# Last four input transposes of FFN-up moved into its first panel, and the fourth pair of weight halves in FFN-down given to other steps

## The chip, the cores and the metric

The kernel runs on one core of one Trainium2 chip. The metric is device time in microseconds, the median of three runs; lower is better. TensorE (PE) multiplies, VectorE (DVE), ScalarE (ACT) and GpSimd (POOL) work on its operands and results, and SyncE (SP) issues most loads.

## The reference, cut to what matters

One decoder layer over 256 tokens of width 2048: a mixer (a pooling part and an RWKV-7 part), an MLP, a gated embedding and a last norm. The change touches the MLP and the step into it:

```python
mix = jnp.concatenate([pool_out, rwkv_out], axis=-1).astype(x.dtype)
x = x + mix @ w_out[i]

h2 = rms_norm(x, mlp_norm[i])
x = x + jnp.square(jax.nn.relu(h2 @ w_ffn_up[i])) @ w_ffn_down[i]   # 2048 -> 8192 -> 2048

gate = jax.nn.sigmoid(rms_norm(x, ple_norm[i]) @ w_ple_gate[i])
x = x + gate * (p[i] @ w_ple_proj[i])
return rms_norm(x, final_norm)
```

## The kernel before, in words

All products are made from float32 values split in two halves, a high one (wh, from an ACT copy into float32r) and a low one (wl, from a DVE subtraction); each product of two split operands takes three matmuls. Weights arrive as raw tiles of 128x1024 (load_raw, line 158, on SP's queue), in two groups of three buffers, are split by ACT and DVE, and then read by TensorE. The tiles wh and wl rotate through three shared buffers each (pool wp). The splits have a high priority (20000), so that they are made as early as buffers and data allow. Order on each engine is decided by a scheduler when the program is built; the code gives program order and priorities. Each engine then works through its own list in that order, and an instruction that waits holds up all behind it on its engine.

**The way into FFN-up.** The output product runs in four column blocks n (gemm_toks, lines 238 to 242); after each, residual (line 1071) adds the block to x on DVE, and h2_part("mlp_norm", n) makes four of the 16 column tiles of h2: for each pair of tiles four transposes on TensorE (line 1134) into half of a two-bank PSUM tile (wide_bank, pool psw with two buffers), and per tile one evacuation on ACT (line 1140, high half) and one on DVE (line 1141, low half). The scale 1/rms is applied later, on the squared result.

**FFN-up** (gemm_wide) runs in 16 panels, eight for each half of the hidden width. A panel has two half panels, and each half panel runs through four quarters kq over the inner width: one raw load, one split (lines 167 and 168), and sixteen matmuls, in groups of two on wh with both halves of h2 (line 1112, 512 columns) and two on wl (line 1117, 256 columns). Quarter kq reads the column tiles 4 kq to 4 kq + 3 of h2. square (lines 1356 to 1358) then evacuates the wide PSUM tile, and begin_sum and activation_sums prepare FFN-down.

**FFN-down** (down_sweep, two sweeps in each half) goes over 16 row blocks kp. Half of them (SEVEN) are done in seven products in place of eight, a Strassen scheme, and are called squares here. A plain block splits its two raw loads by halves_of, giving the pairs a and b. A square has the pair a, a pair b that holds the halves of one raw load (w22) and of a sum from the ring (w1), a pair wad (from the ring less w22, line 1313), and a pair d made from raw weights that were changed in place (line 1315). The ring has two slots; a slot is filled by two DMAs of POOL, the second adding to what the first brought (lines 1232 and 1233), and the first two fills start during FFN-up, in panels 4 and 5.

The pairs a and b get their tiles from half_tiles (line 1266). It counts its calls in turns, and every fourth gets a pair of its own (wh4, wl4, one buffer each), the others the three shared buffers. A sweep has 32 calls, the last one 37. So the fourth call of each sweep, which is pair b of the first square (wh_d_1b, wl_d_1b), has the own pair.

Of the kernel before, what the change touches and what calls it, by code (L numbers as in the profile page):

```python
# [16 lines left out]
T = 256  # L17
# [23 lines left out]
def trunk(  # L41
# [29 lines left out]
    def mm_bank(name):  # L71
        return psm.tile([128, 512], F32, tag="mm", name=name)
# [12 lines left out]
    def col(name, j):  # L85
        o = PARAM_COLS[name] + j
        return par_sb[:, o : o + 1]
# [7 lines left out]
    ident = const.tile([128, 128], F32, name="ident")  # L95
# [53 lines left out]
    def load_raw(src, n, name):  # L149
        own = False  # L150
        if deep:
            deep.append(name)
            own = len(deep) > 5 and len(deep) % 6 < 3
        if own:
            raw = fp.tile([128, 1024], F32, tag="raw2", bufs=3, name=f"raw_{name}")
        else:
            raw = wp.tile([128, 1024], F32, tag="raw", name=f"raw_{name}")
        nc.sync.dma_start(raw[:, 0:n], src)
        return raw

    def split_w(raw, name):

        wh = wp.tile([128, 1024], F32R, tag="wh", name=f"wh_{name}")
        wl = wp.tile([128, 1024], F32R, tag="wl", name=f"wl_{name}")
        with tc.high_priority(20000):
            for a in range(2):
                nc.scalar.activation(wh[:, a * 512 : (a + 1) * 512], raw[:, a * 512 : (a + 1) * 512], AF.Copy)  # L167
            nc.vector.tensor_tensor(wl, raw, wh.bitcast(F32), op=ALU.subtract)  # L168
        return [(t_h, t_l) for t_h, t_l in zip((wh[:, 0:512], wh[:, 512:1024]), (wl[:, 0:512], wl[:, 512:1024]))]

    def split_sb(h_ap, l_ap, src_ap):
        nc.scalar.activation(h_ap, src_ap, AF.Copy)  # L172
        nc.vector.tensor_tensor(l_ap, src_ap, h_ap.bitcast(F32), op=ALU.subtract)
# [111 lines left out]
    def run(gen):  # L285
        for _ in gen:
            pass

    def a8(slot, name, dt=F32):
        return act.tile([128, 2048], dt, tag=f"a{slot}", name=name)  # L290
# [768 lines left out]
    xr = [a8(3 + tt, f"x{tt}") for tt in range(2)]  # L1059
# [7 lines left out]
    def residual(banks, n):  # L1067
        for tt in range(2):
            xs = xr[tt][:, n * 512 : (n + 1) * 512]
            with tc.high_priority(30000):  # L1070
                nc.vector.tensor_tensor(xs, banks[tt], xs, op=ALU.add)
# [23 lines left out]
    def wide_bank(name):  # L1095
        return psw.tile([128, 2, 512], F32, tag="wide", name=name)

    def gemm_wide(src, acts, name, consume):

        for half in range(2):
            bank = wide_bank(f"{name}_w{half}")
            for kq in range(4):
                raw = load_raw(src[half, kq].rearrange("p a n -> p (a n)"), 1024, f"{name}{half}_{kq}")
                for a, (wh, wl) in enumerate(split_w(raw, f"{name}{half}_{kq}")):
                    for b in range(2):
                        k = kq * 4 + 2 * a + b
                        hl = acts(k)
                        cs = [slice(b * 256 + ct * 128, b * 256 + ct * 128 + 128) for ct in range(2)]  # L1110
                        for ct in range(2):
                            nc.tensor.matmul(  # L1112
                                bank[:, ct, :].rearrange("p (s t) -> p s t", s=2), wh[:, cs[ct]], hl,
                                start=k == 0, stop=False, skip_group_check=True,
                            )
                        for ct in range(2):
                            nc.tensor.matmul(  # L1117
                                bank[:, ct, 0:T], wl[:, cs[ct]], hl[:, 0, :], start=False, stop=k == 15, skip_group_check=True
                            )
            consume(half, bank)  # L1120

    def transposed(name):

        hl = fp.tile([128, 2, NK, T], F32R, tag="h2", name=name)
        h, l = hl[:, 0], hl[:, 1]

        def part(norm, n):
            for j2 in range(2 * n, 2 * n + 2):
                if j2 % 2 == 0:
                    b = wide_bank(f"{name}t")  # L1130
                for jj in range(2):
                    j = 2 * j2 + jj
                    for tt in range(2):
                        nc.tensor.transpose(
                            b[:, j2 % 2, jj * T + tt * 128 : jj * T + (tt + 1) * 128], xr[tt][:, j * 128 : (j + 1) * 128], ident
                        )
                for jj in range(2):
                    j = 2 * j2 + jj
                    src = b[:, j2 % 2, jj * T : (jj + 1) * T]
                    nc.scalar.activation(h[:, j, :], src, AF.Copy, scale=col(norm, j))  # L1140
                    nc.vector.scalar_tensor_tensor(
                        l[:, j, :], src, col(norm, j), h[:, j, :].bitcast(F32), op0=ALU.mult, op1=ALU.subtract
                    )

        return part, lambda k: hl[:, :, k, :]

    h2_part, h2 = transposed("h2")
    deep.append("w_out")
    for n in range(4):
        run(gemm_toks(w_out[n], mix, f"o{n}", lambda banks: residual(banks, n), (6, 7, 2, 3)))  # L1150
        h2_part("mlp_norm", n)


    s2 = const.tile([128, 2], F32, name="s2sq")
# [1 line left out]
    def inv_ms():  # L1156
        ss2 = rms_stat(xr, "n2")
        nc.vector.tensor_scalar(s2, ss2, 1.0 / D, NORM_EPS, op0=ALU.mult, op1=ALU.add)
        nc.vector.reciprocal(s2, s2)
        nc.vector.tensor_scalar_mul(ns2, s2, -1.0)  # L1160
# [57 lines left out]
    turns = []  # L1218
# [4 lines left out]
    def begin_sum(after=None):  # L1223

        n = len(begun)
        if not ring:
            ring.append(fp.tile([128, 1024], F32, tag="S", name="ring"))
        if n < len(in_line):
            hf, pair, kp = in_line[n]
            if after is not None:  # L1230
                nc.gpsimd.tensor_copy(slot(n)[:, 0:1], after[:, 0:1])
            nc.gpsimd.dma_start(slot(n), w_down[pair, hf * 16 + kp, 1, :, 1, :])  # L1232
            nc.gpsimd.dma_start(slot(n), w_down[pair, hf * 16 + kp, 0, :, 1, :], accum_op=ALU.add)  # L1233
            begun.append(n)
# [4 lines left out]
    def down_sweep(hf, pair, ys, sboxes, hooks=(), between=None):  # L1239
# [26 lines left out]
        def half_tiles(name):  # L1266

            turns.append(name)
            if len(turns) % 4 == 0:
                return [fp.tile([128, 1024], F32R, tag=f"{hl}4", name=f"{hl}_{name}") for hl in ("wh", "wl")]  # L1270
            return [wp.tile([128, 1024], F32R, tag=hl, name=f"{hl}_{name}") for hl in ("wh", "wl")]

# [20 lines left out]
        for q, kp in enumerate(visits):  # L1293
            if q in hooks:
                hooks[q]()
            y, j = ys[kp // 2], kp % 2 * 512
            a11, a21, a12, a22 = ((y[:, j + i * 128 : j + i * 128 + 128], y[:, 1024 + j + i * 128 : 1152 + j + i * 128]) for i in range(4))
            rx, ry = (panel(kp, c, f"{nm}_{kp}_{c}", 1 if c and kp in seven else 2) for c in range(2))
            if kp in seven:
                i = SEVEN.index(kp)  # L1300
# [27 lines left out]
            if kp == max(seven):  # L1328
                u = fp.tile([128, 512], F32, tag="r", bufs=2, name=f"u{nm}")
# [16 lines left out]
    def ffn_half(hf):  # L1346
        sboxes = {}
        ys = []
        for i in range(8):
            f = hf * 8 + i  # L1350
            y = fp.tile([128, 2048], F32R, tag="y", bufs=8, name=f"y{f}")

            def square(bi, bank):
                r = fp.tile([128, 512], F32, tag="r", bufs=2, name=f"r{f}_{bi}")
                r2 = r.rearrange("p (c t) -> p c t", c=2)
                nc.scalar.activation(r2, bank[:, :, T : 2 * T], AF.Copy)
                nc.vector.tensor_tensor(r2, bank[:, :, 0:T], r2, op=ALU.add)
                nc.vector.scalar_tensor_tensor(r, r, 0.0, r, op0=ALU.max, op1=ALU.mult)  # L1358
                split_sb(y[:, bi * 512 : bi * 512 + 512], y[:, 1024 + bi * 512 : 1024 + bi * 512 + 512], r)
                if f in (4, 5) and bi:  # L1360
                    begin_sum(r)
                if 2 * i + bi in SEVEN:
                    activation_sums(sboxes, 2 * i + bi, r)

            gemm_wide(w_up[f], h2, f"u{f}", square)
            ys.append(y)
            if f == 1:
                inv_ms()

        if hf == 1:  # L1370
            h3_part, h3 = transposed("h3")
            h3_box.append(h3)

        down_sweep(hf, 0, ys, sboxes)
        if hf == 0:
            down_sweep(hf, 1, ys, sboxes)
        else:
            down_sweep(hf, 1, ys, sboxes, {5: keep, 8: keep, 11: keep, 14: keep}, lambda: [h3_part("ple_norm", n) for n in range(2)])
            for n in range(2, 4):
                h3_part("ple_norm", n)  # L1380
# [24 lines left out]
    part = const.tile([128, 1], F32, name="part")  # L1405
# [131 lines left out]
```

## Time and profile before

| | us |
|---|---|
| median of three runs | 1180.53 |
| lowest and highest | 1179.17 and 1183.03 |
| time of the profiled execution | 1182.91 |
| its span, first to last instruction | 1181.1 |
| TensorE, busy (share of the span) | 1162.8 (98%) |
| DVE, ACT, POOL, busy | 877.7, 714.1, 58.5 |
| mean granted clock of TensorE | 0.995 |

Times inside the profile count from the start of its span. A row of a timeline gives start, duration, engine, line, operation, output and inputs, shape, and how often it stands in one row (x2); in square brackets follows how long the engine sat idle before it, and for whom it waited. Numbers of buffers are left out of names (u_w, wh_d_0a), so a name stands for all of a kind. Matmuls overlap: one takes 0.39 us from start to end where the next starts 0.23 us after it. FFN-up's first half runs from 378 to 563 us, FFN-down's first two sweeps to 727, the second half of both to 1072. The windows give for each stretch the busy time and the number of instructions of each engine, then the granted clock of TensorE, the DMA share and the rate.

### The profile page before, as it was taken

To read this page: it belongs to the slowest core of one execution; us is meant where nothing else is said; L and a number is where in the kernel's file an instruction comes from. 1 tells how busy PE (TensorE), PEld (TensorE's weight loads), DVE (VectorE), ACT (ScalarE), POOL (GpSimd) and SP (SyncE) were. 2 spreads that over 40 slices of the span, in tenths; PEclk is the share of its full clock that TensorE was granted. 3 is DMA by queue.
4 is the path that set the end of the run, shared out by engine and by line. 5 is a ranking of instruction groups with operands and counts; after the bars stand their busy time and mean duration, and the time that the engine had idled before them with its cause. 6 is when DMAs were issued, how large, how long until landed. Compare 5 with 4: busy or idle time off the path is not lost.

```text
span 1181.1 us, 17409 instructions
## 1 busy us (share of the span) xinstructions
PE 1162.8 (98%) x6407; PEld 973.1 (82%) x6407; DVE 877.7 (74%) x1194; ACT 714.1 (60%) x1323; POOL 58.5 (5%) x133
## 2 busy tenths in 40 slices
PE   9999999999999999999999999999999999999997
PEld 8787777788887888878888888888888888888886
DVE  8686996954656676757888988676768988897543
ACT  8777858676545565545665664555556665677543
POOL 2100000000000000000110110000000110000000
PEclk9999999999999999989999999999999999999999
DMA  8454443354454555555687686555555886975511
GB/s 294 154 199 144 142 143 109 119 179 161 175 190 171 179 190 191 198 171 204 202 241 244 200 245 233 194 182 194 186 189 174 248 250 228 316 247 190 198 56 72
DMA packets 67253, 224.42 MB, mean 190 GB/s; under 512 B 7712, under 2 KB 8480, under 8 KB 66784
## 3 DMA queue, kind: packets, MB, share of 16 engines
q1 hardware_dynamic: 60240, 207.38, 50.2%
q0 software_dynamic: 6496, 15.21, 5.7%
q8 instruction: 50, 0.82, 0.3%
q10 hardware_dynamic: 432, 0.73, 0.2%
q14 instruction: 35, 0.29, 0.1%
HBM read 221.19 MB, written 2.10 MB: 189 GB/s over the span
## 4 chain that ended last, share of the span: by engine, by line
PE 93%; DVE 3%; DMA 2%; ACT 2%; issue 1%; POOL 0%; SPq 0%; DVEq 0%; POOLq 0%; ACTq 0%
PE u_w L1112 19%; PE u_w L1117 10%; PE d_b L1262 7%; PE d_b L1264 7%; PE d_b L1263 7%; PE d_w L1262 2%; PE d_w L1264 2%; PE d_w L1263 2%; PE gt_b L238 2%; PE gt_b L241 2%; PE gt_b L242 2%; PE o_b L241 1%; PE o_b L242 1%; PE zv_b L238 1%; PE o_b L238 1%; PE zp_b L238 1%
## 5 line engine op out<-in xcount | busy, mean ns | idle before, releaser
L1112 PE MATMUL u_w<-h,wh_u 128*128 128x512 f32 x1024 | 323.8, 398 | 1.8 <-ACT wh_u L167 1.8
L167 ACT ACTIVATE wh_u<-raw_u 128x512 fp32r<-128x512 f32 x256 | 147.4, 623 | 154.9 <-issue 95.5
L168 DVE TENSOR_TENSOR wl_u<-raw_u,wh_u 128x1024 fp32r<-128x1024 f32 x128 | 156.7, 1224 | 104.6 <-ACT wh_u L167 102.9
L1117 PEld LDWEIGHTS u_w<-h,wl_u 128*128 128x128 f32 x1024 | 193.6, 189 | 47.2 <-DVE wl_u L168 1.5
L1117 PE MATMUL u_w<-h,wl_u 128*128 128x256 f32 x1024 | 202.6, 279 | 0.9 <-DVE wl_u L168 0.9
L1112 PEld LDWEIGHTS u_w<-h,wh_u 128*128 128x128 f32 x1024 | 157.0, 190 | 2.0 <-ACT wh_u L167 2.0
L168 DVE TENSOR_TENSOR wl_gt<-raw_gt,wh_gt 128x1024 fp32r<-128x1024 f32 x24 | 29.4, 1224 | 23.2 <-ACT wh_gt L167 23.1
L172 ACT ACTIVATE wad<-ring 128x512 fp32r<-128x512 f32 x29 | 18.2, 629 | 43.1 <-DVE ring L1313 43.1
L167 ACT ACTIVATE wh_gt<-raw_gt 128x512 fp32r<-128x512 f32 x48 | 28.0, 639 | 23.0 <-PE gt_b L242 14.4
L241 PE MATMUL gt_b<-wh_gt,h 128*128 128x512 f32 x96 | 37.3, 389 | 0.0
L242 PE MATMUL gt_b<-wh_gt,h 128*128 128x512 f32 x96 | 37.3, 389 | 0.0
L1315 DVE TENSOR_TENSOR raw_d<-raw_d,ring 128x1024 f32<-128x1024 f32 x29 | 35.5, 1222 | 0.7
L1232 POOL DMA_DIRECT2D ring<-in_w_ffn_down_dram x29 | 16.5, 570 | 356.8 <-DVE r L1358 190.8
L1233 POOL DMA_DIRECT2D ring<-in_w_ffn_down_dram x29 | 25.4, 876 | 110.4 <-DMA ring<-in_w_ffn_down_dram 110.4
L168 DVE TENSOR_TENSOR wl_o<-raw_o,wh_o 128x1024 fp32r<-128x1024 f32 x16 | 19.6, 1223 | 12.9 <-ACT wh_o L167 11.4
L167 ACT ACTIVATE wh_o<-raw_o 128x512 fp32r<-128x512 f32 x32 | 18.4, 623 | 16.3 <-issue 8.5
L167 ACT ACTIVATE wh_zp<-raw_zp 128x512 fp32r<-128x512 f32 x32 | 18.6, 624 | 15.8 <-PE zp_b L242 7.1
L168 DVE TENSOR_TENSOR wl_zk<-raw_zk,wh_zk 128x1024 fp32r<-128x1024 f32 x16 | 19.4, 1220 | 9.8 <-ACT wh_zk L167 9.8
L241 PE MATMUL zv_b<-wh_zv,hTh 128*128 128x512 f32 x64 | 26.0, 406 | 0.0
L241 PE MATMUL zk_b<-wh_zk,hTh 128*128 128x512 f32 x64 | 25.2, 394 | 0.6 <-ACT wh_zk L167 0.6
L241 PE MATMUL zp_b<-wh_zp,hTh 128*128 128x512 f32 x64 | 25.7, 401 | 0.0
L238 PE MATMUL gt_b<-wl_gt,h 128*128 128x512 f32 x96 | 25.7, 389 | 0.0
(927 smaller groups left out, 3007.2 us busy)
## 6 DMA issues: line engine op xcount, KB each, us to landing
raw_u<-in_w_ffn_up_dram SPq DMA_DIRECT2D x128, 512.0 KB, 3.5
raw_d<-in_w_ffn_down_dram SPq DMA_DIRECT2D x99, 512.0 KB, 4.7
ring<-in_w_ffn_down_dram POOLq DMA_DIRECT2D x58, 256.0 KB, 4.5
raw_gt<-in_w_ple_gate_dram SPq DMA_DIRECT2D x24, 512.0 KB, 3.5
raw_zk<-in_w_in_dram SPq DMA_DIRECT2D x16, 512.0 KB, 3.7
raw_zr<-in_w_in_dram SPq DMA_DIRECT2D x16, 512.0 KB, 3.3
raw_zv<-in_w_in_dram SPq DMA_DIRECT2D x16, 512.0 KB, 3.3
raw_zp<-in_w_in_dram SPq DMA_DIRECT2D x16, 512.0 KB, 3.2
```

The lines of the kernel that those rows point to most:

```text
L167: nc.scalar.activation(wh[:, a * 512 : (a + 1) * 512], raw[:, a * 512 : (a + 1) * 512], AF.Copy)
L168: nc.vector.tensor_tensor(wl, raw, wh.bitcast(F32), op=ALU.subtract)
L238: nc.tensor.matmul(banks[tt], ah[:, ts_], halves[a][1], start=False, stop=last)
L241: nc.tensor.matmul(banks[tt], ah[:, ts_], halves[a][0], start=i + a == 0, stop=False)
L242: nc.tensor.matmul(banks[tt], al[:, ts_], halves[a][0], start=False, stop=False)
L1112: nc.tensor.matmul(bank[:, ct, :].rearrange("p (s t) -> p s t", s=2), wh[:, cs[ct]], hl, start=k == 0, stop=False, skip_group_check=True,)
L1117: nc.tensor.matmul(bank[:, ct, 0:T], wl[:, cs[ct]], hl[:, 0, :], start=False, stop=k == 15, skip_group_check=True)
L1233: nc.gpsimd.dma_start(slot(n), w_down[pair, hf * 16 + kp, 0, :, 1, :], accum_op=ALU.add)
L1262: nc.tensor.matmul(banks[n], ah, wh, start=first, stop=False)
L1263: nc.tensor.matmul(banks[n], ah, wl, start=False, stop=False)
L1264: nc.tensor.matmul(banks[n], al, wh, start=False, stop=last)
L1315: nc.vector.tensor_tensor(t43, t43, t2.unsqueeze(1).to_broadcast([128, 2, 512]), op=ALU.subtract)
```

## The change

There are two edits. The first takes the last block of transposes out of the loop over n and calls it from gemm_wide, in the very first half panel of FFN-up, between the first and the second quarter; there it uses two plain one-bank tiles of the pool psm (mm_bank) in place of one wide tile. The second lets half_tiles give its own pair to calls 1, 5, 9 and so on in place of 4, 8, 12.

```diff
-    def gemm_wide(src, acts, name, consume):
+    def gemm_wide(src, acts, name, consume, first=None):
         for half in range(2):
             bank = wide_bank(f"{name}_w{half}")
             for kq in range(4):
+                if first is not None and half == 0 and kq == 1:
+                    first()
                 raw = load_raw(src[half, kq].rearrange("p a n -> p (a n)"), 1024, f"{name}{half}_{kq}")
...
-        def part(norm, n):
+        def part(norm, n, pair=None):
             for j2 in range(2 * n, 2 * n + 2):
-                if j2 % 2 == 0:
+                if pair is not None:
+                    b = pair[j2 % 2].unsqueeze(1)
+                elif j2 % 2 == 0:
                     b = wide_bank(f"{name}t")
+                at = 0 if pair is not None else j2 % 2
...
     for n in range(4):
         run(gemm_toks(w_out[n], mix, f"o{n}", lambda banks: residual(banks, n), (6, 7, 2, 3)))
-        h2_part("mlp_norm", n)
+        if n < 3:
+            h2_part("mlp_norm", n)
+
+    def h2_rest():
+        h2_part("mlp_norm", 3, [mm_bank(f"h2t{i}") for i in range(2)])
...
             turns.append(name)
-            if len(turns) % 4 == 0:
+            if len(turns) % 4 == 1:
                 return [fp.tile([128, 1024], F32R, tag=f"{hl}4", name=f"{hl}_{name}") for hl in ("wh", "wl")]
...
-            gemm_wide(w_up[f], h2, f"u{f}", square)
+            gemm_wide(w_up[f], h2, f"u{f}", square, h2_rest if f == 0 else None)
```

What the scheduler makes of it is shown at three places. In the changed kernel the lines behind 1098 have other numbers: 1137 is the transpose, 1285 the split in halves_of, 1363 the evacuation in square.

On TensorE, from the last matmul of the output product (o_b) into FFN-up (u_w), before; wh_u_0 and wl_u_0 are the halves of the first quarter, wh_u_1 those of the second, and h2t is the transposes' tile:

```order
L238 MATMUL o_b_3652<-wl_o_3_3713,mp_3213 128x512
L1134 MATMUL h2t<-ident,x_2724 128x128
L1112 MATMUL u_w_3751<-h_3359,wh_u_0_3754 128x512 x2
L1117 MATMUL u_w_3751<-h_3359,wl_u_0_3755 128x256
L1134 MATMUL h2t<-ident,x_2725 128x128
```

And the same place now:

```order
L238 MATMUL o_b_3652<-wl_o_3_3713,mp_3213 128x512
L1112 MATMUL u_w_3734<-h_3359,wh_u_0_3737 128x512 x2
L1117 MATMUL u_w_3734<-h_3359,wl_u_0_3738 128x256 x2
...
L1137 MATMUL h2t_3758<-ident,x_2724 128x128
L1137 MATMUL h2t_3758<-ident,x_2725 128x128
...
L1137 MATMUL h2t_3759<-ident,x_2724 128x128
L1137 MATMUL h2t_3759<-ident,x_2725 128x128
...
L1112 MATMUL u_w_3734<-h_3359,wh_u_1_3778 128x512 x2
```

Before, the first transpose stood ahead of FFN-up's first matmul and the eight were strewn into its first seventeen; now the sixteen matmuls of the first quarter come first, then all eight transposes, then the second quarter. On ACT and DVE the eight evacuations stand behind the split of the fourth quarter; before, half of them stood ahead of it.

On ACT, in panel 4 of FFN-up's first half, before; wh_d_1b<-ring is the split of the ring's sum for square 1, y and S are FFN-down's other operands:

```order
L167 ACTIVATE wh_u_0_4911<-raw_u_0_4909 128x512 x2
L172 ACTIVATE S_4690<-s_4801 128x512
L167 ACTIVATE wh_u_1_4934<-raw_u_1_4932 128x512 x2
L172 ACTIVATE wh_d_1b<-ring 128x512
L167 ACTIVATE wh_u_2_4957<-raw_u_2_4955 128x512 x2
L1356 ACTIVATE r_0_4902<-u_w_4809 128x512
```

And now, in the last half panel, where that split went:

```order
L167 ACTIVATE wh_u_0_5328<-raw_u_0_5326 128x512 x2
L1285 ACTIVATE wh_d_0a<-raw_d_0_0_5430 128x512 x2
L172 ACTIVATE S_5011<-s_5218 128x512
L167 ACTIVATE wh_u_1_5351<-raw_u_1_5349 128x512 x2
...
L1285 ACTIVATE wh_d_0b<-raw_d_0_1_5432 128x512 x2
L1285 ACTIVATE wh_d_1a<-raw_d_1_0_5468 128x512 x2
L172 ACTIVATE wh_d_1b<-raw_d_1_1_5470 128x512
L172 ACTIVATE wh_d_1b<-ring 128x512
L1363 ACTIVATE r_1_5418<-u_w_5325 128x512
L172 ACTIVATE wad_1_5472<-ring 128x512
L1285 ACTIVATE wh_d_1d<-raw_d_1_0_5468 128x512 x2
```

The ring's split moved from panel 4 to behind the last splits of FFN-up, where both halves of wh_d_1b and wad now follow each other; wh_d_0a moved the other way, into the last half panel. DVE's list follows ACT's in both places. The second half of FFN has the same order at its end; there the ring's split had stood in the first panel. On SP the loads stand as before up to FFN-down, where one later load passes raw_d_1_1; POOL's list is the same.

More of the change, by code (lines that the diff above doesn't have):

```diff
@@ L1134, in part @@
                         nc.tensor.transpose(
-                            b[:, j2 % 2, jj * T + tt * 128 : jj * T + (tt + 1) * 128], xr[tt][:, j * 128 : (j + 1) * 128], ident
+                            b[:, at, jj * T + tt * 128 : jj * T + (tt + 1) * 128], xr[tt][:, j * 128 : (j + 1) * 128], ident
                         )
@@ L1138, in part @@
                     j = 2 * j2 + jj
-                    src = b[:, j2 % 2, jj * T : (jj + 1) * T]
+                    src = b[:, at, jj * T : (jj + 1) * T]
                     nc.scalar.activation(h[:, j, :], src, AF.Copy, scale=col(norm, j))
```

## Prediction

> **What bounds the kernel now.** I read the page first, then the list of TensorE's waits, then TensorE's timeline and its windows around each wait in the part that the change touches.
>
> ```profile
> span 1181.1 us, 17409 instructions
> PE 1162.8 (98%) x6407; PEld 973.1 (82%) x6407; DVE 877.7 (74%) x1194; ACT 714.1 (60%) x1323; POOL 58.5 (5%) x133
> PEclk9999999999999999989999999999999999999999
> ```
>
> TensorE is busy 98% of the span, so only what makes it idle or slow can be won. One slice of 40 does not show full clock: the 18th, about 502 to 531 us, in the middle of FFN-up. The waits of TensorE that lie behind the output product are these three:
>
> ```profile
> PE u_w L1112 <- ACT wh_u L167: 1.8, 1, 1.8
> ...
> PE u_w L1117 <- DVE wl_u L168: 0.9, 1, 0.9
> ...
> PE h2t L1134 <- DVE x L1071: 0.6, 1, 0.6
> ```
>
> The first two are one event. TensorE's timeline shows it; the groups of two L1112 and two L1117 repeat through all of FFN-up:
>
> ```profile
> 497.69 0.63 PE L1112 MATMUL u_w<-h,wh_u 128*128 128x512 f32 x2
> ...
> 506.75 0.63 PE L1112 MATMUL u_w<-h,wh_u 128*128 128x512 f32 x2
> 507.22 0.39 PE L1117 MATMUL u_w<-h,wl_u 128*128 128x256 f32 x2
> 509.37 0.87 PE L1112 MATMUL u_w<-h,wh_u 128*128 128x512 f32 x2 [1.76 <-ACT wh_u L167]
> 511.15 0.79 PE L1117 MATMUL u_w<-h,wl_u 128*128 128x256 f32 x2 [0.91 <-DVE wl_u L168]
> 511.74 1.05 PE L1112 MATMUL u_w<-h,wh_u 128*128 128x512 f32 x2
> ...
> 516.77 0.63 PE L1112 MATMUL u_w<-h,wh_u 128*128 128x512 f32 x2
> ```
>
> From 497.69 to 506.75 lie 13 groups, 0.697 us each. From 511.74 the same pairs take 1.05 in place of 0.63. The windows of one microsecond give the granted clock (third number from the right):
>
> ```profile
> 508.00:509.00 1.00, 0.00 (x0) 0.00 (x0) 0.17 (x1) 0.83 (x2) 0.00 (x0) 1.00 0.00 0
> ...
> 510.00:511.00 1.00, 0.24 (x1) 0.00 (x0) 1.00 (x1) 1.00 (x3) 0.00 (x0) 0.50 0.00 0
> ...
> 515.00:516.00 1.00, 1.00 (x4) 0.82 (x4) 0.38 (x1) 0.56 (x2) 0.00 (x0) 0.50 0.93 352
> ...
> 517.00:518.00 1.00, 1.00 (x7) 0.86 (x6) 0.85 (x1) 0.00 (x0) 0.00 (x0) 1.00 0.80 315
> ```
>
> So TensorE stands, and then runs at half rate until about 516.7. The whole event costs more than the 2.7 us that the waits name. The next group was due at 506.75 + 0.697 = 507.45, and the sixth from there at 507.45 + 5 x 0.697 = 510.93. It came at 516.77: **5.84 us lost**. Who held TensorE up is seen on ACT:
>
> ```profile
> 499.10 1.15 ACT L167 ACTIVATE wh_u<-raw_u 128x512 fp32r<-128x512 f32 x2 [1.11 <-issue]
> 508.17 0.63 ACT L172 ACTIVATE wh_d_1b<-ring 128x512 fp32r<-128x512 f32 x1 [7.91 <-DMA ring<-in_w_ffn_down_dram]
> ```
>
> ACT stands 7.91 us at a split that FFN-down needs some 60 us later: the sum in the ring for square 1, whose DMA has not landed. The wh_u splits that TensorE needs are queued behind it.
>
> **The change part by part.** *The rotation.* half_tiles gave its own pair of tiles (wh4, wl4) to every fourth call. The fourth call of a half is square 1's second pair, the one that takes the ring. The own pair had been free since before, so nothing but the ring's DMA held this split back, and at its high priority it went into the middle of FFN-up. Now the own pair goes to the first call (wh_d_0a), and the ring's split takes a shared tile that the last FFN-up matmul must free. ACT's order shows it gone from panel 4. I take the whole 5.84 us off: before it ACT's conversions run ahead of TensorE by more than a quarter panel, and no other row of TensorE's waits follows.
>
> What comes in its place lies at two spots, in each half. First, wh_d_0a now stands before the last half panel, and ACT waits there for the load of raw_d_0_0:
>
> ```profile
> 543.57 0.33 SPq L158 DMA_DIRECT2D raw_d<-in_w_ffn_down_dram  x1
> ...
> 546.76 1.15 ACT L167 ACTIVATE wh_u<-raw_u 128x512 fp32r<-128x512 f32 x2 [1.16 <-issue]
> ...
> DMA to landing us min/median/max: 2.5/4.6/8.5
> ```
>
> The last row is that of the raw_d loads. ACT is free at 547.91; the load, issued at 543.57, lands at 548.2 by the median. ACT waits 0.3 us. Behind it stand the S split and the next wh_u, together 2.75 us to its end; TensorE wants that quarter at 555.1 and its wl half at 555.56. So the landing may be as late as 551.6, 8.0 us after the issue, before TensorE notices. Cost zero, bounds 0 and 0.5 us (a load of 8.5). On SP the early use of raw_d_0_0 frees its buffer, and one later load (raw_d_2_1, in the second half raw_d_3_0) passes raw_d_1_1; its buffer is free then, so nothing is held behind it.
>
> Second, square 1's splits, its subtraction from the ring and the wad split, which had been done during FFN-up, now stand behind the last FFN-up matmul. The rows there, before:
>
> ```profile
> 563.48 1.15 ACT L1278 ACTIVATE wh_d_1a<-raw_d 128x512 fp32r<-128x512 f32 x2 [1.64 <-issue]
> ...
> 565.80 0.68 DVE L1357 TENSOR_TENSOR r<-u_w,r 128x512 f32<-128x512 f32 x1
> 566.40 1.21 DVE L1315 TENSOR_TENSOR raw_d<-raw_d,ring 128x1024 f32<-128x1024 f32 x1
> ...
> 569.27 1.22 DVE L1279 TENSOR_TENSOR wl_d_1d<-raw_d,wh_d_1d 128x1024 fp32r<-128x1024 f32 x1
> ...
> 572.53 0.39 PE L1263 MATMUL d_b<-wl_d_1d,y 128*128 128x512 f32 x1
> ```
>
> wl_d_1d ends at 570.49 and is wanted at 572.53: 2.0 us to spare. In the new order ACT begins the first of the two wh_d_1b splits at 563.48 (wh_d_1a moves one step earlier), so DVE begins at 564.16. Five half-width operations (wl_d_1b twice, r, ring, r again) follow at 0.60 us each, the step from 565.80 to 566.40: L1315 at 567.16. With 1.14 us for a full one, wad stands at 568.30, wl_d_2a at 568.90, wl_d_1d at 570.04, done at 571.26. It is 1.27 us early instead of 2.0. Cost zero; 1.27 us is what a slip may use up, twice in the kernel. POOL's refill of that ring slot for square 4 waits for the last reader, wad at 568.98 in place of L1315:
>
> ```profile
> 568.17 0.56 POOL L1232 DMA_DIRECT2D ring<-in_w_ffn_down_dram  x1 [40.65 <-DVE raw_d L1315]
> 571.50 0.89 POOL L1233 DMA_DIRECT2D ring<-in_w_ffn_down_dram  x1 [2.76 <-DMA ring<-in_w_ffn_down_dram]
> ...
> 579.89 0.62 ACT L172 ACTIVATE wh_d_4b<-ring 128x512 fp32r<-128x512 f32 x1
> ```
>
> Its second transfer then starts near 572.9 in place of 571.5 and has 7 us to land before the split at 579.89 wants it, itself five microseconds ahead of TensorE: no cost.
>
> At the way back from FFN-down to FFN-up the shared tiles are one fewer: the three last splits of the sweep sit in them.
>
> ```profile
> 724.20 1.15 ACT L167 ACTIVATE wh_u<-raw_u 128x512 fp32r<-128x512 f32 x2 [2.41 <-PE d_b L1264]
> ...
> 726.67 0.61 PE L1112 MATMUL u_w<-h,wh_u 128*128 128x512 f32 x2
> ```
>
> What starts at 724.20, when TensorE has read wh_d_15a, is now the third quarter's split; in the new order it is the second's, wanted at 726.67 + 4 x 0.697 = 729.46. It and its DVE half are done by 727: no cost. At the end of the kernel transposes of h3 and the gate's splits change places; TensorE has no wait there now, and I count nothing.
>
> *The transposes.* Around the start of FFN-up, before:
>
> ```profile
> 376.68 1.07 PE L238 MATMUL o_b<-wl_o,mp 128*128 128x512 f32 x4
> ...
> 378.30 0.33 PE L1134 MATMUL h2t<-ident,x 128*128 128x128 f32 x1 [0.56 <-DVE x L1071]
> ...
> 384.83 0.62 PE L1112 MATMUL u_w<-h,wh_u 128*128 128x512 f32 x2
> ```
>
> The four L238 start 0.227 apart (1.07 less the 0.39 of one, over 3), so the next matmul was due at 377.59. It came at 378.30, because eight transposes (two per 128 columns) read x, and x waits for DVE's residual. The row at 384.83 begins the third quarter. In the new order the first quarter stands in front: its h comes from the first column block, its splits are those that the matmuls behind 378.30 use now, so it starts at 377.59. What eight transposes in one row cost is read off the same thing in h3:
>
> ```profile
> 1061.08 0.40 PE L1264 MATMUL d_b<-wh_d_14a,y 128*128 128x512 f32 x1
> 1061.31 1.04 PE L1134 MATMUL h3t<-ident,x 128*128 128x128 f32 x8
> 1062.11 0.47 PE L1262 MATMUL d_b<-wh_d_14a,y 128*128 128x512 f32 x1
> ```
>
> 1062.11 less 1061.31 is 0.80 us. The third quarter then starts at 377.59 + 2 x 4 x 0.697 + 0.80 = 383.97, and **0.86 us** is won. The eight evacuations that follow (four on ACT, four on DVE, in two banks) stand behind the split of the fourth quarter on both engines, and are wanted at 383.97 + 2.79 = 386.76, the first pair then, the last one 2 us later. ACT can begin them at 381.4, DVE at 382.7; at about half a microsecond each they end before 386.6 even if each waits for the other. The cover is the second and third quarter; were it gone, 0.86 is what there is to lose.
>
> *The sum.* 5.84 + 0.86 = 6.70 us of a profiled execution of 1182.91 us (span 1181.1): 1176.2. The median of the runs shown is 1180.53, 2.4 us less, and 6.70 off it gives 1173.8. The three runs lie 3.9 us apart, and the profiled one is near the slowest. If the event of 508 us is what differs between runs, the timed ones have less to win and 1176.2 is the end; if not, 1173.8. I put it between, at 1175.0.
>
> **The rivals.** *The half rate belongs to some runs only.* For it: the waits are 1.76 and 0.91 us, and the list also has this one, at 37.54 us, where the clock of the window stays at 1.00:
>
> ```profile
> PE wagT L464 <- POOL wband L130: 1.7, 1, 1.7
> ```
>
> Without the half rate the rest of the first group would have started at 511.15 all the same, the second at 511.38 and the sixth at 511.38 + 4 x 0.697 = 514.17, 3.24 us late. The gain is 3.24 + 0.86 = 4.1 us: 1176.4 from the median. Against it: the page's profile is one of few, and it shows the stretch. The Trainium skill's page "TensorE: Matmul & The Clock Gate", Part 1 (the HAM clock gate), says that the clock falls to half after an idle window of some 3.4 us, and that the windows run freely, so that the slow stretch of one kernel varies from run to run. By that rule this stall is too short to be sure of a slow stretch, and the change would be worth the smaller sum; this trace differs, with 0.50 after waits of 1.76 and 0.91 us.
>
> *Square 1 comes late.* If a semaphore or an operation more than I counted takes the 1.27 us, TensorE waits for wl_d_1d in both halves. Three microseconds of delay would cost 2 x 1.7 = 3.4 us and leave 3.3 of the gain: 1177.2. For it: DVE is the fuller engine there. Against it: every step is a duration from a row.
>
> *Slower: the new early split blocks ACT as the old one did.* The place is wh_d_0a before the last half panel. TensorE notices when raw_d_0_0 takes over 8.0 us; a wait like the old one, 7.9 us on ACT, needs a load of 12.2 us. Twice 5.84 in place of once, less 0.86, is 5.0 us more than now: 1185.5. Against it: the slowest of the raw_d loads took 8.5.
>
> *The change doesn't do what it says.* The third quarter's or the fourth's h comes late and the 0.86 is lost again: 1175.9, the rotation alone.
>
> **How the numbers follow.** Forecast 0.75; half rate in some runs only 0.11; square 1 late 0.06; transposes without gain 0.05; slower 0.03. A change of 0.3%, 3.5 us, is about what a measurement of this kernel can tell from none, so faster means below 1177.0. The forecast and the lost transposes lie there, and most of the half-rate case (1176.4): 0.85. Same: the rest of that case and square 1: 0.12. Slower 0.03. Low end: 1173.8 less the 1.3 us by which the lowest run lies under the median, 1172.5. High end: 1176.4 plus the same 1.3, 1177.7, which takes in square 1 late.
>
> **What would show it.** Right: no ACT wait for the ring in FFN-up and no window below clock 1.00 between 380 and 1170; 0.697 us per group from 377.6 on; 5.6 us and eight transposes' 0.8 from the last L238 to the third quarter; wl_d_1d over a microsecond ahead of its matmul; a span near 1174.4. Wrong: a TensorE wait at either FFN-down start, an ACT wait for raw_d of more than 3.7 us, or a half-rate stretch at another place.

## The result, and the profile after

The changed kernel takes 1176.76 us (median of 13 runs, 1175.94 to 1179.02). The kernel before takes 1180.53 us (13 runs, 1176.46 to 1183.76). The ratio is 0.9961, with a 95% interval of 0.995 to 0.9972: 4.6 us less, between 3.3 and 5.9; the two medians lie 3.8 us apart. The forecast was 1175.0 us in a range of 1172.5 to 1177.7.

The head of the page of the changed kernel; its profiled execution took 1177.08 us:

```profile
span 1175.1 us, 17401 instructions
PE 1160.5 (99%) x6407; PEld 971.5 (83%) x6407; DVE 877.2 (75%) x1194; ACT 713.3 (61%) x1323; POOL 57.2 (5%) x133
PEclk9999999999999999999999999999999999999999
```

No slice has a digit below 9 now. TensorE's windows of ten microseconds where it had stood and run at half rate (behind the span come PE, PEld, DVE, ACT and POOL, then the granted clock):

```profile
500.00:510.00 10.00, 10.00 (x60) 8.76 (x59) 6.09 (x7) 5.21 (x10) 0.51 (x1) 1.00 0.71 218
510.00:520.00 10.00, 10.00 (x59) 8.71 (x59) 7.67 (x12) 5.40 (x10) 0.98 (x3) 1.00 0.63 224
```

TensorE's timeline from the last four matmuls of the output product to the third quarter of FFN-up:

```profile
376.50 1.07 PE L238 MATMUL o_b<-wl_o,mp 128*128 128x512 f32 x4
377.40 0.62 PE L1112 MATMUL u_w<-h,wh_u 128*128 128x512 f32 x2
...
380.18 1.04 PE L1137 MATMUL h2t<-ident,x 128*128 128x128 f32 x8
380.98 0.70 PE L1112 MATMUL u_w<-h,wh_u 128*128 128x512 f32 x2
...
383.84 0.63 PE L1112 MATMUL u_w<-h,wh_u 128*128 128x512 f32 x2
```

FFN-up begins without a wait, the eight transposes take 0.80 us (380.98 less 380.18), and the third quarter starts 7.34 us behind the row at 376.50. Before it was 384.83 less 376.68, 8.15: 0.81 us are won.

Where did the rest come from? The two spans differ by 6.0 us. Place by place, from the timelines of both: the mixer in front ended 0.18 us earlier, the transposes gave 0.81, FFN-up from its third quarter to FFN-down's first matmul 5.86. Then two pieces are given back: 0.71 in FFN-down's first sweep, and 0.23 behind the last sweep. The first of these is TensorE's only wait behind the output product:

```profile
PE d_b L1270 <- DVE wl_d_9d L1286: 0.4, 1, 0.4
```

ACT, POOL and TensorE of the changed kernel there, one fence for each:

```profile
583.16 0.63 ACT L172 ACTIVATE wh_d_6b<-ring 128x512 fp32r<-128x512 f32 x1 [2.52 <-DMA ring<-in_w_ffn_down_dram]
```

```profile
575.42 0.87 POOL L1240 DMA_DIRECT2D ring<-in_w_ffn_down_dram  x1 [3.68 <-DMA ring<-in_w_ffn_down_dram]
```

```profile
605.63 0.39 PE L1269 MATMUL d_b<-wh_d_9d,y 128*128 128x512 f32 x1
606.37 0.50 PE L1270 MATMUL d_b<-wl_d_9d,y 128*128 128x512 f32 x1 [0.35 <-DVE wl_d_9d L1286]
```

The ring's second transfer for square 6 was issued at 575.42, and the split that needs it could start at 583.16 only, 7.7 us later. DVE, the fuller engine in FFN-down, doesn't catch up before square 9, where TensorE meets it.

### The profile page after: what moved, and what is told of

Its sections match the earlier page's. It is cut to its first block, busy times and chain, and to the rows that moved or that the text cites. A ratio compares the mean times of both kernels' runs of the same rounds, so it can differ in the third digit from the quotient of the medians.

```text
span 1175.1 us, 17401 instructions
## 1 busy us (share of the span) xinstructions
PE 1160.5 (99%) x6407; PEld 971.5 (83%) x6407; DVE 877.2 (75%) x1194; ACT 713.3 (61%) x1323; POOL 57.2 (5%) x133
## 4 chain that ended last, share of the span: by engine, by line
PE 95%; DVE 2%; ACT 1%; issue 0%; DMA 0%; POOL 0%; SPq 0%; DVEq 0%; POOLq 0%
PE u_w L1112 20%; PE u_w L1117 10%; PE d_b L1270 7%; PE d_b L1269 7%; PE d_b L1271 7%; PE d_w L1270 2%; PE d_w L1269 2%; PE d_w L1271 2%; PE gt_b L241 2%; PE gt_b L242 2%; PE gt_b L238 2%; PE zk_b L241 1%; PE zk_b L242 1%; PE o_b L238 1%; PE o_b L241 1%; PE o_b L242 1%
## 5 line engine op out<-in xcount | busy, mean ns | idle before, releaser
L238 PE MATMUL gt_b<-wl_gt,h 128*128 128x512 f32 x96 | 25.8, 389 | 0.0
L168 DVE TENSOR_TENSOR wl_zv<-raw_zv,wh_zv 128x1024 fp32r<-128x1024 f32 x16 | 19.4, 1218 | 8.2 <-ACT wh_zv L167 7.3
```

Source lines behind the costliest of these rows:

```text
L238: nc.tensor.matmul(banks[tt], ah[:, ts_], halves[a][1], start=False, stop=last)
```

## The experiments

All columns but the last two come from the profiles (us). "Stretch" runs on TensorE from the row of the last four L238 of the output product to the first matmul of FFN-down; in the changed kernel it is 556.61 less 376.50. What a stop costs is the stretch less that of a kernel with the same transposes and no stop (180.93 with those of before, 180.11 with the new ones).

| kernel | stretch | ACT's wait | cost of the stop | at half rate in FFN-up | median, runs | ratio to before |
|---|---|---|---|---|---|---|
| before | 186.78 | 7.91 | 5.85 | 6.8 | 1180.53, 13 | |
| changed | 180.11 | none | | none | 1176.76, 13 | 0.9961 (0.995 to 0.9972) |
| before again | 185.36 | 7.59 | 4.43 | 3.4 | 1181.64, 12 | 1.0009 (0.9995 to 1.0024) |
| transposes alone | 181.82 | 6.26 | 1.71 | none | 1179.17, 12 | 0.9995 (0.998 to 1.001) |
| rotation alone | 180.93 | none | | none | 1177.85, 12 | 0.9984 (0.9971 to 0.9997) |
| one DMA | 180.94 | 2.73 | none | none | 1177.01, 12 | 0.9975 (0.9963 to 0.9988) |
| changed again | 180.12 | none | | none | 1177.20, 9 | 0.9966 (0.9953 to 0.9978) |
| split tied to panel 6 | 180.12 | none | | none | 1176.72, 6 | 0.9958 (0.9944 to 0.9972) |
| three DMAs | 188.84 | 9.52 | 7.91 | 6.8 | 1185.40, 10 | 1.0032 (1.002 to 1.0045) |
| late raw load | 181.88 | 5.71 | 1.77 | none | 1179.68, 10 | 0.998 (0.9969 to 0.9992) |

The third to the sixth kernel ran on one chip, beside 35 runs of the kernel before (median 1181.38). The last four ran on another, beside 26 (1181.58).

### The kernel before, again

No edit.

> The kernel before, unchanged, to see span and granted clock of every run. My theory: ACT's wait at the ring's split is a DMA landing time and differs from run to run; the long runs (1182 to 1184 us) show a mean granted clock of about 0.995 (6.8 us at half rate are 0.003 of the span), the short ones (1176 to 1177 us) 0.998 as in the changed kernel, and in those the stop is nearly absent. Rival (every run has the same stop of 5.84 us, and the runs differ by something else): clock 0.995 in all runs, and no relation of span and clock.

The profile caught another stop than the first one. ACT, TensorE, and the windows:

```profile
507.46 0.63 ACT L172 ACTIVATE wh_d_1b<-ring 128x512 fp32r<-128x512 f32 x1 [7.59 <-DMA ring<-in_w_ffn_down_dram]
```

```profile
506.36 0.63 PE L1112 MATMUL u_w<-h,wh_u 128*128 128x512 f32 x2
...
508.66 0.74 PE L1112 MATMUL u_w<-h,wh_u 128*128 128x512 f32 x2 [1.44 <-ACT wh_u L167]
510.44 0.80 PE L1117 MATMUL u_w<-h,wl_u 128*128 128x256 f32 x2 [1.04 <-DVE wl_u L168]
...
513.55 0.63 PE L1112 MATMUL u_w<-h,wh_u 128*128 128x512 f32 x2
```

```profile
510.00:511.00 1.00, 0.56 (x2) 0.56 (x3) 0.99 (x2) 0.65 (x2) 0.00 (x0) 0.53 0.00 0
511.00:512.00 1.00, 1.00 (x5) 0.81 (x4) 0.98 (x2) 0.25 (x1) 0.00 (x0) 0.50 0.51 86
512.00:513.00 1.00, 1.00 (x5) 0.90 (x4) 1.00 (x2) 1.00 (x3) 0.00 (x0) 0.50 0.91 356
513.00:514.00 1.00, 1.00 (x5) 0.83 (x5) 1.00 (x2) 0.42 (x1) 0.00 (x0) 0.76 0.41 131
```

A mean clock of 0.53 is 0.94 us at half rate, 0.76 is 0.48 us: 0.94 + 1 + 1 + 0.48 = 3.42 us. The first profile had 0.18 us in the window from 509, six whole ones, and 0.64 us in that from 516 (0.68): 6.82. The stop is almost the same (7.59 against 7.91 us on ACT), the half rate lasts half as long, and the cost is 4.43 in place of 5.85 us.

Each run's mean clock tells something of the half rate in it, since 3.42 us at half rate are 0.0014 of the span. Not all of it lies at the stop. The clock also falls behind TensorE's last matmul and stays at half to the end of the span, for 3.4 to 6.1 us in the ten profiles; there it delays no matmul. The longest such end is that of the kernel with the transposes alone, whose span is 1176.3 us:

```profile
1170.00:1171.00 1.00, 0.00 (x0) 0.00 (x0) 0.93 (x5) 0.75 (x4) 0.00 (x0) 0.58 0.00 0
...
1175.00:1176.00 1.00, 0.00 (x0) 0.00 (x0) 0.00 (x0) 0.00 (x0) 0.00 (x0) 0.50 0.00 0
```

With an end of 3.4 to 6.1 us, a run without any other half rate has a mean clock of 0.999 to 0.997, one with one piece of 3.42 us has 0.997 or 0.996, and one with two has 0.996 or less. These are all runs of the two kernels that list their clock:

| mean clock of the run | before, 73 runs | changed, 22 runs |
|---|---|---|
| 0.998 or 0.999 | 22, mean 1178.90 us | 15, mean 1176.61 us |
| 0.997 | 27, 1181.27 | 5, 1178.46 |
| 0.993 to 0.996 | 24, 1183.06 | 2, 1178.91 |

So the runs do differ by the half rate, as expected. By this reckoning 22 of 73 had none, 24 had at least one piece, and the middle run, at 0.997, had one piece of 3.4 us at most, not two. A piece needn't come from this stop: 7 of the 52 runs of kernels without it (the changed kernel, the rotation alone, one DMA, the tied split) have 0.996 as well. The rival, one stop of 5.84 us in every run, falls, by the 4.43 us of this profile and by the clocks. "The stop is nearly absent" in the short runs was not what I found: with no half rate they are still 2.3 us longer than the changed kernel's (1178.90 less 1176.61). The transposes are 0.8 of it; the other 1.5 I put down to the stop itself.

### The transposes alone

The changed kernel with half_tiles as before.

```diff
-            if len(turns) % 4 == 1:
+            if len(turns) % 4 == 0:
```

> Only the transposes' edit; half_tiles as before. My theory: 0.8 us less than before (1179.7 against 1180.53 us), the third quarter starts 7.3 us behind the last four matmuls of the output product in place of 8.15, and the profile still has ACT's wait for the ring at wh_d_1b in panel 4, with a TensorE wait and a stretch of clock 0.50 behind it where that wait is over 6 us. Rival (the transposes carry the gain, the ring's stop doesn't matter in the median): 1176.8 us.

ACT and TensorE in this kernel, and one of its windows:

```profile
505.92 0.63 ACT L172 ACTIVATE wh_d_1b<-ring 128x512 fp32r<-128x512 f32 x1 [6.26 <-DMA ring<-in_w_ffn_down_dram]
```

```profile
506.16 0.63 PE L1112 MATMUL u_w<-h,wh_u 128*128 128x512 f32 x2
...
507.13 0.73 PE L1112 MATMUL u_w<-h,wh_u 128*128 128x512 f32 x2
508.91 0.50 PE L1117 MATMUL u_w<-h,wl_u 128*128 128x256 f32 x2 [1.04 <-DVE wl_u L168]
```

```profile
509.00:510.00 1.00, 1.00 (x7) 0.91 (x8) 0.96 (x2) 0.12 (x1) 0.00 (x0) 1.00 0.25 41
```

The ring landed sooner here. The first group behind the stop came 0.27 us late (507.13, due at 506.16 + 0.697), TensorE stood 1.04 us more in the middle of it, and the clock stayed at 1.00, though I had expected half rate behind any wait of over 6 us. The stop cost 1.71 us. In the median this kernel is 2.2 us under the 1181.38 of before and 2.0 above the 1177.20 of the changed one, which ran on another chip; its ratio leaves anything from 1.2 us lost to 2.4 us won, the 0.8 us of the timeline among it. The transposes don't carry the gain alone.

### The rotation alone

The kernel before with the other turn.

```diff
-            if len(turns) % 4 == 0:
+            if len(turns) % 4 == 1:
```

> Only the rotation; transposes as before. My theory: all but 0.8 us of the gain, 1177.6 us, no ACT wait for the ring in FFN-up, no window under clock 1.00 there, a TensorE wait of about 0.56 us at the transposes of x as before. Rival: 1179.7 us or more.

TensorE's only wait behind the output product is the one at the transposes:

```profile
PE h2t L1134 <- DVE x L1071: 0.6, 1, 0.6
```

It took 1177.85 us: right within 0.3, and the stretch is 0.82 us longer than with both edits, the transposes' share once more. FFN-down's first sweep, which was 82.09 us long in the changed kernel's profile (556.61 to 638.70) and 81.38 before, is 81.44 here.

### One DMA in the first sum

The kernel before; square 1 of the first sweep gets half of its sum.

```diff
-            nc.gpsimd.dma_start(slot(n), w_down[pair, hf * 16 + kp, 0, :, 1, :], accum_op=ALU.add)
+            if n > 0:
+                nc.gpsimd.dma_start(slot(n), w_down[pair, hf * 16 + kp, 0, :, 1, :], accum_op=ALU.add)
```

> The kernel before, with the second of the two DMAs of the very first ring sum left out (so that square 1 of the first sweep uses half of its sum). The ring's split stays hoisted into FFN-up, with the own pair as before. My theory (the landing of two DMAs in a row is what held ACT 7.91 us): ACT waits 5 us or less, ahead of which it has about 6 us of lead, so TensorE has no wait in FFN-up and the time is that of the rotation alone, 1177.6 us. Rival (it is the place of the split that costs, not the DMA): a TensorE wait stays there and the time is 1180 us.

The split stayed in panel 4, a quarter earlier still, and ACT waits for the one transfer only:

```profile
499.97 0.63 ACT L172 ACTIVATE wh_d_1b<-ring 128x512 fp32r<-128x512 f32 x1 [2.73 <-DMA ring<-in_w_ffn_down_dram]
```

TensorE doesn't notice: the stretch is 180.94 us, as with the rotation, and the median 1177.01. So the split that the scheduler had moved into FFN-up costs nothing by itself. What cost was that ACT met it before the second transfer had landed.

### The split tied to panel 6

The changed kernel's transposes, the own pair with the ring's split as before, and one column copied ahead of it, so that the scheduler can't put it before the second half of panel 6.

```diff
-            if len(turns) % 4 == 1:
+            if len(turns) % 4 == 0:
...
                     split_sb(*w22, ry[:, 0:512])
+                    if (hf, pair, kp) == in_line[0]:
+                        nc.scalar.activation(wh[:, 512:513], ys[6][:, 512:513], AF.Copy)
                     split_sb(*w1, p1)
```

> The transposes' edit, with the own pair left to the fourth call (the ring's split), but that split tied to the sixth panel's y by a copy of one column ahead of it on ACT, so that it stands in front of the last panel and not in the one in which the ring's transfers begin. Theory (what costs is only that ACT meets the ring's split before its transfers have landed): no ACT wait for the ring, no TensorE wait in FFN-up, about 1176.5 us, the same as the changed kernel within 0.1%. Rival (the own pair on the ring's split costs by itself, or the rotation gains more than the stop): 1178 us or more.

ACT at the new place of the split:

```profile
540.71 0.20 ACT L1320 ACTIVATE wh_d_1b<-y 128x1 fp32r<-128x1 f32 x1
540.94 0.64 ACT L172 ACTIVATE wh_d_1b<-ring 128x512 fp32r<-128x512 f32 x1
```

No wait for the ring, no wait of TensorE behind the output product, the same stretch as the changed kernel, and 1176.72 us. The rotation is thus worth what the lost stop is worth, and no more. From the changed kernel's 1177.20 on the same chip this can't be told apart (the intervals overlap). Its profile shows half rate at another place, in the mixer, behind a stop that the kernel before has too (the waits of TensorE, then its windows):

```profile
PE wagT L464 <- ACT wagS L459: 1.6, 1, 1.6
```

```profile
38.00:39.00 1.00, 0.86 (x7) 0.80 (x8) 0.80 (x3) 0.41 (x2) 0.86 (x3) 0.85 0.89 360
39.00:40.00 1.00, 1.00 (x4) 0.81 (x4) 0.50 (x2) 0.98 (x2) 0.86 (x5) 0.50 0.04 16
...
42.00:43.00 1.00, 1.00 (x6) 0.82 (x5) 0.93 (x5) 0.08 (x1) 0.00 (x0) 0.94 0.00 0
```

That is 0.30 + 3 + 0.12 = 3.42 us again, and FFN-up begins 2 us later than in the changed kernel's profile. The changed kernel's longer runs may have it from there: the two at a mean clock of 0.996 have a piece somewhere, the five at 0.997 may have one. None of them was profiled.

### The changed kernel, again

No edit.

> The changed kernel, unchanged, a second look, on the same chip as the three that follow. In its profile on record FFN-down's first sweep is 0.7 us longer than in the kernel before, behind a ring transfer that landed 7.7 us after its issue. Theory (chance: the rotation issues the ring's refills about 1 us later and so leaves a slow transfer less room, but most transfers are in time): that sweep takes 81.4 us here as in the rotation alone, and the median stays at 1176.8 us. Rival (the change always costs the 0.7 us there): the sweep takes 82 us again.

The first sweep takes 81.43 us (556.36 to 637.79), TensorE has no wait behind the output product, and the ratio to before is 0.9966 (0.9953 to 0.9978). The 0.7 us belong to one execution's slow transfer; the three other profiles with the rotation don't have them.

### Three DMAs in the first sum

The kernel before, with one operand added twice, so that square 1 of the first sweep uses another sum.

```diff
             nc.gpsimd.dma_start(slot(n), w_down[pair, hf * 16 + kp, 0, :, 1, :], accum_op=ALU.add)
+            if n == 0:
+                nc.gpsimd.dma_start(slot(n), w_down[pair, hf * 16 + kp, 0, :, 1, :], accum_op=ALU.add)
```

> The kernel before with a third DMA into the first ring sum (which adds one operand twice, so that square 1 of the first sweep uses a wrong sum). ACT's wait gets longer by about 5 us less the 1 to 3 us by which its split moves back. Theory (TensorE loses what ACT's wait exceeds a lead of 4.6 us, and half rate on top in some of the runs): ACT waits 10 to 12 us, TensorE loses 6 to 8 us without the half rate and up to 3.5 us more with it, 1184 to 1188 us. Theory of a stop that always brings the same half-rate stretch: 6 to 7 us of clock 0.50 in the profile, and a clock of 0.995 or less in every run. Rival (ACT's wait isn't what TensorE waits for): 1181 us as before.

ACT and TensorE:

```profile
512.17 0.63 ACT L172 ACTIVATE wh_d_1b<-ring 128x512 fp32r<-128x512 f32 x1 [9.52 <-DMA ring<-in_w_ffn_down_dram]
```

```profile
509.14 0.63 PE L1112 MATMUL u_w<-h,wh_u 128*128 128x512 f32 x2
...
513.85 1.22 PE L1112 MATMUL u_w<-h,wh_u 128*128 128x512 f32 x2 [3.85 <-ACT wh_u L167]
516.04 0.79 PE L1117 MATMUL u_w<-h,wl_u 128*128 128x256 f32 x2 [0.97 <-DVE wl_u L168]
```

ACT waited 9.52 us, a little less than forecast, and the stop cost 7.91 us. Without half rate the second group would have come 0.23 us behind 516.04; it was due two groups behind 509.14, at 510.53. So 5.7 us belong to the stop and 2.2 to the clock. The median of 1185.40 is within what my theory gave. The theory of a fixed stretch has its 6 to 7 us in this profile. It also said a clock of 0.995 or less in every run, and five of the ten show 0.996, but the profiled run with its 6.84 us is one of these five, so the clocks don't decide. What speaks against a fixed stretch is the kernel before, with 6.8 us in one profile and 3.4 in the other.

### A late raw load

The changed kernel, the first raw load of FFN-down's first sweep made twice.

```diff
             rx, ry = (panel(kp, c, f"{nm}_{kp}_{c}", 1 if c and kp in seven else 2) for c in range(2))
+            if (hf, pair, q) == (0, 0, 0):
+                nc.gpsimd.dma_start(rx, w_down[pair, hf * 16 + kp, 0, :, 0:2].rearrange("p r n -> p (r n)"))
```

> The changed kernel with the first raw load of FFN-down's first sweep made twice (the same data again by GpSimd's queue behind the first), so that the split that was hoisted in the ring's place gets its data about 5 us later; the order puts that split one quarter later. Theory (the place has room: TensorE notices only a landing past about 547.5 us on the changed kernel's clock): ACT waits 2.5 to 5 us for the load, TensorE 1 us at most, 1176.8 to 1178 us. Rival (the new hoisted split is as dear as the old one once its load is late): TensorE loses 3 us or more, 1180 us.

POOL, ACT and TensorE:

```profile
543.85 0.55 POOL L1307 DMA_DIRECT2D raw_d<-in_w_ffn_down_dram  x1 [21.05 <-DMA raw_d<-in_w_ffn_down_dram]
```

```profile
551.71 1.15 ACT L1285 ACTIVATE wh_d_0a<-raw_d 128x512 fp32r<-128x512 f32 x2 [5.71 <-DMA raw_d<-in_w_ffn_down_dram]
```

```profile
555.31 0.50 PE L1117 MATMUL u_w<-h,wl_u 128*128 128x256 f32 x2 [1.14 <-DVE wl_u L168]
```

The second load took 7.8 us, ACT waited longer than I had allowed, and TensorE lost 1.77 us. That is between the two expectations, and the median of 1179.68 is nearer to the rival's. But the median isn't the stop alone: the profiled span is 4.2 us longer than that of the changed kernel on the same chip (1178.4 and 1174.2), and 2.4 of it had come up before FFN-up, where the mixer had a piece of half rate. Where its load is late, the new early split is about as dear as the old one was: 1.77 us at a wait of 5.71, against 1.71 at 6.26 with the transposes alone, both without half rate there. With the one load of the changed kernel ACT doesn't wait there at all.

## Why the prediction was right or wrong

**The cause: right.** FFN-up's stop came from ACT at the ring's split, waiting for the second of two transfers. It goes when the split goes (rotation), when the transfer goes (one DMA), and when the split only moves behind the landing (tied to panel 6); it grows with a third transfer.

**The size of the stop: the step that failed.** "I take the whole 5.84 us off" holds for the profiled execution, which lost 5.85. It isn't the loss of the timed runs. The two profiles of the kernel before show 5.85 and 4.43, and that of the transposes alone 1.71. In the middle run of the kernel before there is one piece of half rate at most, not two. I had seen that the three runs lay 3.9 us apart and that the profiled one was long, and had 1176.2 for the case that this stop is what differs between runs. It is, in large part; yet I put the forecast between that and 1173.8. The measured 1176.76 lies beside the rival of half rate in some runs only (a gain of 4.1 us, 1176.4), to which I gave 0.11. The range holds it because its high end was set from that rival; the step that gave 1175.0 doesn't explain it.

**The transposes: right.** 0.81 us in place of 0.86, by a third quarter 7.34 us behind the last L238 where 7.29 was forecast. The evacuations made nobody wait.

**The early split of wh_d_0a: right.** These are ACT's rows in the changed kernel:

```profile
541.02 1.16 ACT L1285 ACTIVATE wh_d_0a<-raw_d 128x512 fp32r<-128x512 f32 x2
542.08 0.61 ACT L172 ACTIVATE S<-s 128x512 fp32r<-128x512 f32 x1
```

There is no wait. The late raw load tries the limit. Its first load was issued at 538.87 us and its data came at 551.71, and TensorE lost 1.77, so it begins to lose at 551.71 - 1.77 - 538.87 = 11.1 us behind the issue. The split stands one quarter later there; my 8.0 us plus the 2.79 of a quarter is 10.8. The slower rival had its mechanism right where a load is late, and in none of the profiles of the kernels with the rotation did that load come late by itself.

**Square 1: right.** wl_d_1d was to be done 1.27 us ahead of its matmul. DVE and TensorE:

```profile
563.13 1.22 DVE L1286 TENSOR_TENSOR wl_d_1d<-raw_d,wh_d_1d 128x1024 fp32r<-128x1024 f32 x1
```

```profile
565.71 0.39 PE L1270 MATMUL d_b<-wl_d_1d,y 128*128 128x512 f32 x1
```

It ends at 564.35, 1.36 us ahead.

**The ring's refill: right for square 4, not followed to its end.** I had the refill's second transfer 9.4 us behind FFN-down's start, where it was 9.1 (8.0 before), and no cost at square 4. The delay of about a microsecond runs on to the next slots. For square 6 the second transfer starts 18.8 us behind FFN-down's start (575.42 less 556.61), where before it was 17.8 (581.28 less 563.46):

```profile
581.28 0.88 POOL L1233 DMA_DIRECT2D ring<-in_w_ffn_down_dram  x1 [3.26 <-DMA ring<-in_w_ffn_down_dram]
```

The split that takes it comes about 24 us behind that start where nothing is late. A transfer thus has about 5 us in place of 6, and the one of 7.7 us cost 0.71 us on TensorE. In the other profiles with the rotation that sweep takes 81.4 us.

**The end of the kernel: 0.2 us missed.** I counted nothing for the transposes of h3 and the gate's splits. From the last wh_d_15b to the last row of the gate product (gt_b) it is 77.6 us in the four profiles with the rotation, and 77.4 in the six without; which step takes the 0.2 is not shown.

**The sum.** 6.70 us were forecast for the profiled execution; 6.67 had been won when FFN-down began. The slow transfer and the end took 0.94 back, and the front gave 0.18.

## What to carry to other kernels

A split, a copy or a conversion that a scheduler hoists because its buffer is free and its priority high is only as early as its data. Look on each in-order engine for what waits on a transfer ahead of work that is due sooner, and either tie it to a later point or give the free buffer to another step. Before the loss of a stop that hangs on a transfer is taken off a median, take a second profile or the clocks of several runs: the one at hand may be a long one. Take the half rate behind the last matmul off such a clock first.

## What the runs showed of the hardware

The half rate comes in pieces of one length. Behind the stops it lasted 3.42 us (kernel before, again), 6.82 (before), 3.42 (in the mixer of the tied kernel), and none at all (transposes alone, late raw load). In the kernel with three DMAs, the two outer windows and six whole ones between them give 0.26 + 6 + 0.58 = 6.84:

```profile
513.00:514.00 1.00, 0.15 (x1) 0.15 (x1) 1.00 (x2) 1.00 (x3) 0.00 (x0) 0.87 0.00 0
514.00:515.00 1.00, 1.00 (x2) 0.35 (x2) 0.96 (x3) 0.44 (x2) 0.00 (x0) 0.50 0.00 0
...
520.00:521.00 1.00, 1.00 (x6) 0.87 (x5) 0.00 (x0) 0.72 (x2) 0.00 (x0) 0.71 0.62 242
```

The page's row of digits is too coarse for one piece: the tied kernel's shows 9 in every slice.

The falls lie on a grid, too. In the kernel before the clock fell at 509.82 us (the 0.18 us in the window from 509) and, behind the last matmul, at 1175.42 (the window from 1175 has 0.71). That is 665.60 us, or 195 pieces of 3.4133 us. In the four other profiles with a fall inside the kernel the distance is 195 (before, again), 332 (tied), 195 (three DMAs) and 333 (late load) such pieces, each within 0.02 us. The Trainium skill's page "TensorE: Matmul & The Clock Gate", Part 1, has a window of 3413 ns that runs freely and doesn't start with the kernel. The traces agree with that length, and with a phase that changes from run to run. The page also asks for a whole idle window before the clock falls. Here less was enough: the clock fell behind stops of 0.97, 1.44, 1.61 and 1.76 us, and 3.85 is the only one that fills a window. Cut along the grid, the kernel before and its second profile show:

```profile
506.40:509.82 3.42, 1.66 (x10) 1.17 (x8) 0.69 (x1) 1.65 (x4) 0.00 (x0) 1.00 0.03 7
509.82:513.23 3.41, 2.50 (x9) 1.89 (x8) 3.33 (x4) 2.31 (x6) 0.00 (x0) 0.50 0.24 85
513.23:516.64 3.41, 3.41 (x11) 2.83 (x11) 2.17 (x4) 2.04 (x4) 0.00 (x0) 0.50 0.66 238
```

```profile
506.65:510.07 3.42, 1.31 (x6) 0.62 (x4) 1.60 (x2) 2.61 (x6) 0.00 (x0) 1.00 0.01 2
510.07:513.48 3.41, 3.04 (x10) 2.65 (x11) 3.37 (x6) 2.25 (x5) 0.00 (x0) 0.50 0.49 157
513.48:516.89 3.41, 3.41 (x21) 2.96 (x21) 2.42 (x2) 1.15 (x2) 0.00 (x0) 1.00 0.73 220
```

From FFN-up to the end, 13 windows in the ten profiles stand ahead of a fall, and TensorE was busy 0 to 1.66 us in each; the emptiest window that no fall followed had 2.12 us (late raw load, 1168.21 to 1171.63). A window at half rate with 2.34 (three DMAs) or 2.50 us of work was followed by a second one; with 3.04 or more it wasn't. So whether a stop brings no piece, one or two depends on how its waits fall into the windows. With the transposes alone the two windows from 504.56 had 3.19 and 2.47 us of work, and the clock stayed. Where between 1.66 and 2.12 us the limit lies no run shows. In the mixer, where eight matmuls of one column stand ahead of the stop, the busy time doesn't tell: a window with 2.44 us was followed by a fall (late load, a stop of 0.97 us), and one with 1.76 us wasn't (before, a stop of 1.66 us).

The two transfers of one ring sum are in a row and vary with the run: ACT's wait for them was 6.26, 7.59 and 7.91 us in three profiles with the same order of work around them. The lead that ACT has over TensorE varies little. The stop's cost without the half rate is 1.71 us at a wait of 6.26 (transposes alone), 2.9 at 7.59 (before again: a second group at 510.44 + 0.23, due at 506.36 + 2 x 0.697), and 3.24 at 7.91 (before). The differences are 4.55, 4.7 and 4.67 us. With the blocking split one quarter later they are 3.8 (three DMAs) and 3.9 (late raw load).
